# The first seven rows of a row-sum kernel, loaded in two transfers over 32 and 96 partitions

## The chip, the core and the metric

The kernel runs on one core of a Trainium2 chip. The core has 128 on-chip memory partitions and several engines with instruction streams of their own: VectorE (DVE in the profile), ScalarE (ACT), GpSimd (POOL), TensorE (PE, not used here) and SyncE (SP), which issues most transfers. Transfers are carried out by 16 DMA engines. The metric is the time of one execution on the device in microseconds (us); for a single core this is the core's own time.

## The reference

The input `x` is 32 x 512 x 1024 float32 (67.1 MB), the output the sum over its last axis, 32 x 512 float32 (65.5 KB).

```python
def reference(x: np.ndarray) -> np.ndarray:
    return np.sum(x, axis=-1).astype(np.float32)
```

So every element is read once and added once; there are 16,384 row sums of 1,024 elements.

## The kernel before

**Tiling.** The 16,384 rows are spread over the 128 partitions, 128 rows (`J`) for each. They form two blocks: `x_b`, of which each partition has 112 consecutive rows (`LONG`), and `x_a`, of which each has 16 (`BIG`). `rows_from(j, n)` gives the rows `j` to `j + n - 1` of every partition; since the rows of one partition follow each other in memory, one load of `n` rows takes one run of `n` x 4,096 bytes for each partition. Row sums are collected in `sums` (128 x 128) and stored in three parts at the end.

**Stages.** Twelve loads go through three buffers of sixteen rows each (`inpool`, `bufs=3`):

1. the first load: rows 0 to 6 of `x_b` over all 128 partitions, 28,672 B for each (`FIRST = 7`, line 212);
2. seven loads of sixteen rows, 65,536 B for each partition (loop of lines 215 to 224): first the block `x_a`, then rows 16 to 111 of `x_b`;
3. the rest of the first sixteen rows: six rows (line 227), two rows (line 228), and one row in two pieces of 560 and 464 elements (lines 236 and 237).

The first load and the first six of stage 2 are reduced by a single VectorE instruction each (`vec`, line 152). For the last sixteen-row load and the six and two rows, VectorE and ScalarE share the rows: VectorE folds a row's halves (`halves`, line 166), ScalarE sums while copying (`act`, line 179). VectorE alone sums the last row from its two pieces.

**What sets the order.** The schedule is written by hand (`tc.manual_schedule()`): each engine runs its instructions in program order. All loads are issued by SyncE, by line 191 in the helper `rows` and by lines 236 and 237. What each waits for:

- The very first SyncE load is moved by `issue_first_load_at_entry` ahead of the barrier with which the program begins; it must wait for nothing.
- The next load (`k == 0`) is held until `ready`, a small ScalarE activation (line 206), has ended; the code gives as a reason that no second load is to be issued while the first one's descriptors are made.
- The load of `k == 1` is held until the first reduction (`first`) has ended.
- Each later load waits until its buffer is free, that is until the load and the reduction that used it three loads before are done.

`order_waits` sorts the waits of instructions that have several, and `wait_for_the_store_at_the_clear` moves the wait for the last store; neither is touched by the change.

Of the kernel before, what the change touches and what calls it, by code (L numbers as in the profile page):

```python
# [100 lines left out]
@with_exitstack  # L101
def kernel(
    ctx: ExitStack,
    tc: tile.TileContext,
    x: bass.AP,
    out: bass.AP,
):
    nc = tc.nc
    nc.at_finalize(issue_first_load_at_entry)
    nc.at_finalize(order_waits)  # L110
    nc.at_finalize(wait_for_the_store_at_the_clear)
    fp32 = mybir.dt.float32
    P = 128
    batch, seq, dim = x.shape
    rows = batch * seq
    J = rows // P
    BIG = 16

    LONG = J - BIG
    rows_in = x.flatten_outer_dims()
    rows_out = out.rearrange("b s -> (b s)")
    x_a = rows_in[: P * BIG].rearrange("(p j) d -> p j d", p=P)
    x_b = rows_in[P * BIG :].rearrange("(p j) d -> p j d", p=P)
    out_a = rows_out[: P * BIG].rearrange("(p j) -> p j", p=P)
    out_b = rows_out[P * BIG :].rearrange("(p j) -> p j", p=P)


    def rows_from(j, n):
        return x_b[:, j : j + n, :] if j < LONG else x_a[:, j - LONG : j - LONG + n, :]

    last = 0
    FIRST = 7
    pieces = (560, 464)
    LINE = 64

    with (
        tc.tile_pool(name="small", bufs=1) as smallpool,  # L140
        tc.tile_pool(name="in", bufs=3) as inpool,
        tc.tile_pool(name="unread", bufs=4, space=bass.MemoryType.PSUM) as upool,
        tc.tile_pool(name="stage", bufs=1) as stpool,
        tc.manual_schedule(),
    ):


        seed = smallpool.tile([P, LINE // 2], fp32)
        sums = stpool.tile([P, J], fp32)

        def vec(dst, src):
            return nc.vector.tensor_reduce(  # L152
                out=dst, in_=src, axis=mybir.AxisListType.X, op=mybir.AluOpType.add
            )

        def hold(inst, until, reason):
            tc.add_manual_dep(
                inst.ins,
                until.ins.name,
                mybir.DependencyInfo(mybir.DependencyClass.Sync, mybir.DependencyReason.DATA),  # L160
                reason=reason,
            )

        def halves(dst, src):
            n = src.shape[-1] // 2
            return nc.vector.tensor_tensor_reduce(  # L166
                out=src[:, :n],
                in0=src[:, :n],
                in1=src[:, n:],
                scale=1.0,  # L170
                scalar=0.0,
                op0=mybir.AluOpType.add,
                op1=mybir.AluOpType.add,
                accum_out=dst,
            )

        def act(dst, src, n):
            unread = upool.tile([P, dim], fp32)
            nc.scalar.activation(  # L179
                out=unread[:, :n],  # L180
                in_=src,
                func=mybir.ActivationFunctionType.Copy,
                accum_out=dst,
            )

        sums_of = []

        def rows(t, a, n, j, n_act, pairs=False):
            nv = n - n_act
            block = t[:, a * dim : (a + n) * dim].rearrange("p (n d) -> p n d", d=dim)  # L190
            load = nc.sync.dma_start(out=block, in_=rows_from(j, n))  # L191
            if pairs:
                for q in range(nv):
                    sums_of.append(halves(sums[:, j + q : j + q + 1], block[:, q, :]))
            else:
                sums_of.append(vec(sums[:, j : j + nv], block[:, :nv, :]))
            for q in range(nv, n):
                act(sums[:, j + q : j + q + 1], block[:, q, :], dim)
            return load

        def store(eng, dst, j0, j1):
            return eng.dma_start(out=dst, in_=sums[:, j0:j1])

        nc.vector.memset(seed[:, :1], 0.0)  # L204
        unread = upool.tile([P, dim], fp32)
        ready = nc.scalar.activation(  # L206
            out=unread[:, :1], in_=seed[:, :1], func=mybir.ActivationFunctionType.Copy
        )

        j = last  # L210
        t = inpool.tile([P, BIG * dim + LINE], fp32)
        rows(t, 0, FIRST, j, 0)
        first = sums_of[-1]
        wholes = [LONG, *range(BIG, LONG, BIG)]
        for k, at in enumerate(wholes):
            t = inpool.tile([P, BIG * dim + LINE], fp32)
            if k < len(wholes) - 1:
                load = rows(t, 0, BIG, at, 0)
            else:
                rows(t, 0, BIG, at, 7, pairs=True)  # L220
            if k == 0:
                hold(load, ready, "no second load while the first one's descriptors are made")
            if k == 1:
                hold(load, first, "no descriptors of later loads while the first ones start")

        t = inpool.tile([P, BIG * dim + LINE], fp32)
        rows(t, FIRST, 6, j + FIRST, 2, pairs=True)
        two = rows(t, FIRST + 6, 2, j + FIRST + 6, 1, pairs=True)
        a = BIG - 1

        j += a
        c, width = pieces
        whole = t[:, a * dim + c : BIG * dim + 2]
        nc.vector.memset(whole[:, width + 1 :], 0.0)  # L234
        part = t[:, a * dim : a * dim + c]
        nc.sync.dma_start(out=part, in_=rows_from(j, 1)[:, 0, :c])  # L236
        nc.sync.dma_start(out=whole[:, :width], in_=rows_from(j, 1)[:, 0, c:])
        late = "its packets come behind those of the loads"
        hold(store(nc.scalar, out_b[:, BIG:], BIG, LONG), two, late)
        hold(store(nc.scalar, out_a, LONG, J), two, late)  # L240
        halves(whole[:, width : width + 1], part)
        halves(sums[:, j : j + 1], whole)
        store(nc.sync, out_b[:, :BIG], 0, BIG)
# [30 lines left out]
```

## Time and profile before

| what | value |
|---|---|
| three runs | 161.17, 161.21, 161.32 us; median 161.21 us |
| profiled execution | span 159.5 us from the first to the last instruction (the profile gives no other time for this execution) |
| VectorE busy | 120.6 us, 76% of the span |
| ScalarE busy | 12.1 us, 8% |
| mean transfer rate over the span | 421 GB/s |
| bytes read from device memory | 67.11 MB |
| first load, issue to landing | 11.0 us |

How to read it. Times in the profile start at the first instruction, which here is the issue of the first load. "SPq" is the queue of SyncE, "PEq" that of TensorE; L191 is line 191 of the kernel. An instruction in the timeline has its start, its length and, in brackets, how long its engine was idle before it and what ended that idle time. The chain of waits follows the work that ended last back from the end, at each step to what released it. A window lists the busy time of each engine in a stretch, the share of the DMA engines and the rate in GB/s. Busy shares are averages over the whole span; what bounds a stage is read from the wait that ends last in it.

### The profile page before, as it was taken

Reading aid. Unit: us, or ns where it says so; the run is one execution under the profiler, and the core shown is the slowest. Engines: PE = TensorE matmul, PEld = TensorE weight load, DVE = VectorE, ACT = ScalarE, POOL = GpSimd, SP = SyncE. Lnnn points to the kernel's source line nnn. Section 1 sums busy time; section 2 is a strip of 40 time slices with the busy share of each in tenths; the row PEclk is TensorE's granted clock in tenths of the full one; section 3 lists DMA queues with packets and bytes.
Section 4 is the critical chain, followed back from the end, with each engine's and each line's share of the span. In section 5 each row is a group of like instructions: output and inputs, shape, how many; then the busy total and the mean of one; then the engine's idle time right before and its main releaser. Section 6 shows DMA issues by size and latency. Waiting matters only on the chain.

```text
span 159.5 us, 135 instructions
## 1 busy us (share of the span) xinstructions
DVE 120.6 (76%) x41; ACT 12.1 (8%) x22; POOL 0.2 (0%) x4
## 2 busy tenths in 40 slices
DVE  0029600499995999769996899949999499994955
ACT  3000000000000000000000000000000000003993
POOL 0000000000000000000000000000000000000000
DMA  8899899699699699699699798996996996996993
GB/s 302 388 493 526 362 427 526 296 493 526 263 526 526 263 526 526 263 526 493 296 526 444 345 526 378 411 526 296 493 526 263 526 526 263 526 526 265 425 382 128
DMA packets 2160, 67.18 MB, mean 421 GB/s; under 512 B 624, under 2 KB 752, under 8 KB 880
## 3 DMA queue, kind: packets, MB, share of 16 engines
q1 hardware_dynamic: 1872, 67.12, 97.8%
q10 hardware_dynamic: 288, 0.06, 0.2%
HBM read 67.11 MB, written 0.07 MB: 421 GB/s over the span
## 4 chain that ended last, share of the span: by engine, by line
DMA 71%; DVE 27%; SPq 1%; issue 0%; DVEq 0%
DMA t<-in_x_dram 71%; DVE sums L152 26%; SPq L191 0%; SPq L236 0%; DVE t L166 0%; DVEq L269 0%
## 5 line engine op out<-in xcount | busy, mean ns | idle before, releaser
L152 DVE TENSOR_REDUCE sums<-t 128x16 f32<-128x16384 f32 (+1 forms) x7 | 110.9, 15849 | 32.3 <-DMA t<-in_x_dram 32.3
L179 ACT ACTIVATE unread<-t 128x1024 f32<-128x1024 f32 x10 | 10.1, 1011 | 144.3 <-DMA t<-in_x_dram 144.3
L166 DVE CUSTOM_DVE_ANT_0 t<-t 128x512 f32<-128x512 f32 (+2 forms) x16 | 9.6, 654 | 4.0 <-DMA t<-in_x_dram 4.0
L179 ACT ACTIVATION_READ_ACCUMULATOR unread<-t 128x1 f32 x10 | 1.9, 188 | 0.0
L206 ACT ACT_TABLE_LOAD x1 | 1.3, 1283 | 0.8 <-PEq L258 0.8
L166 DVE DVE_READ_ACCUMULATOR2_ANT sums<- 128x1 f32 x15 | 1.2, 82 | 0.0
L204 DVE MEMSET seed<- 128x1 f32 x1 | 0.1, 59 | 0.8 <-PEq L258 0.8
L206 ACT ACTIVATE unread<-seed 128x1 f32<-128x1 f32 x1 | 0.2, 174 | 0.0
L258 POOL MEMSET const-bfloat16-1.0<- 128x1 bf16 x1 | 0.1, 102 | 0.0
L258 POOL MEMSET const-uint8-127<- 128x1 uint8 x1 | 0.1, 102 | 0.0
L258 POOL MEMSET const-float32-0.0<- 128x1 f32 x1 | 0.1, 99 | 0.2 <-issue 0.2
L258 POOL MEMSET const-float32-1.0<- 128x1 f32 x1 | 0.1, 99 | 0.0
L166 DVE DVE_READ_ACCUMULATOR2_ANT t<- 128x1 f32 x1 | 0.1, 83 | 0.0
L234 DVE MEMSET t<- 128x1 f32 x1 | 0.1, 59 | 0.0
## 6 DMA issues: line engine op xcount, KB each, us to landing
t<-in_x_dram SPq DMA_DIRECT2D x1, 3584.0 KB, 11.0
t<-in_x_dram SPq DMA_DIRECT2D x1, 3072.0 KB, 28.7
t<-in_x_dram SPq DMA_DIRECT2D x1, 1024.0 KB, 30.7
t<-in_x_dram SPq DMA_DIRECT2D x1, 280.0 KB, 31.0
t<-in_x_dram SPq DMA_DIRECT2D x1, 232.0 KB, 31.1
t<-in_x_dram SPq DMA_DIRECT2D x7, 40.7
out_dram<-sums ACTq DMA_DIRECT2D x1, 48.0 KB, 1.6
out_dram<-sums ACTq DMA_DIRECT2D x1, 8.0 KB, 1.6
```

Source lines behind the costliest of these rows:

```text
L152: return nc.vector.tensor_reduce(out=dst, in_=src, axis=mybir.AxisListType.X, op=mybir.AluOpType.add)
L166: return nc.vector.tensor_tensor_reduce(out=src[:, :n], in0=src[:, :n], in1=src[:, n:], scale=1.0, scalar=0.0, op0=mybir.AluOpType.add, op ...
L179: nc.scalar.activation(out=unread[:, :n], in_=src, func=mybir.ActivationFunctionType.Copy, accum_out=dst,)
L204: nc.vector.memset(seed[:, :1], 0.0)
L206: ready = nc.scalar.activation(out=unread[:, :1], in_=seed[:, :1], func=mybir.ActivationFunctionType.Copy)
L234: nc.vector.memset(whole[:, width + 1 :], 0.0)
L258: nc = _bacc.Bacc("TRN2", target_bir_lowering=False, num_devices=1)
```

## The change

The first load, of rows 0 to 6, is split by partitions: one load over partitions 0 to 31 and another over 32 to 127, with the same 28,672 B for each partition. The first of the two is now the one that is issued at the entry. The second takes over the wait for `ready` that the first sixteen-row load (`k == 0`) had, and that load now has no wait of its own and is issued directly behind. The reduction of the seven rows stays one VectorE instruction over all 128 partitions and waits for both loads. The hold of `k == 1` on this reduction stays.

```diff
         j = last
         t = inpool.tile([P, BIG * dim + LINE], fp32)
-        rows(t, 0, FIRST, j, 0)
-        first = sums_of[-1]
+        block = t[:, : FIRST * dim].rearrange("p (n d) -> p n d", d=dim)
+        few = 32
+        nc.sync.dma_start(out=block[:few], in_=rows_from(j, FIRST)[:few])
+        other = nc.sync.dma_start(out=block[few:], in_=rows_from(j, FIRST)[few:])
+        hold(other, ready, "no second load while the first one's descriptors are made")
+        first = vec(sums[:, j : j + FIRST], block)
+        sums_of.append(first)
         wholes = [LONG, *range(BIG, LONG, BIG)]
         for k, at in enumerate(wholes):
             t = inpool.tile([P, BIG * dim + LINE], fp32)
...
                 rows(t, 0, BIG, at, 7, pairs=True)
-            if k == 0:
-                hold(load, ready, "no second load while the first one's descriptors are made")
             if k == 1:
                 hold(load, first, "no descriptors of later loads while the first ones start")
```

SyncE's order of issue is then: the load over 32 partitions (entry), the load over 96 partitions (after `ready`), the sixteen-row loads, and everything behind as before.

## The prediction

> **What bounds the kernel now.** I read the chain of waits first, because it says which work ends last at each step; then the first microseconds of the timeline and of the windows, because the change lies there; then the DMA queues and SyncE's own waits. The chain (start us, duration us, what), in part:
>
> ```profile
> 0.00 11.01 DMA t<-in_x_dram
> ...
> 11.03 7.63 DVE sums L152
> ...
> 18.68 30.92 DMA t<-in_x_dram
> ...
> 126.16 31.13 DMA t<-in_x_dram
> ...
> 157.32 0.40 DVE t L166
> ```
>
> The share of 26.4% that this chain gives to L152 misleads: it names the reductions because a load's issue waits for them, while the timeline shows VectorE waiting for data ahead of every one of them:
>
> ```profile
> 0.00 19.48 SPq L191 DMA_DIRECT2D t<-in_x_dram  x4
> ...
> 2.06 0.17 ACT L206 ACTIVATE unread<-seed 128x1 f32<-128x1 f32 x1
> 11.03 7.62 DVE L152 TENSOR_REDUCE sums<-t 128x7 f32<-128x7168 f32 x1 [10.14 <-DMA t<-in_x_dram]
> 30.30 17.22 DVE L152 TENSOR_REDUCE sums<-t 128x16 f32<-128x16384 f32 x1 [11.65 <-DMA t<-in_x_dram]
> ...
> 49.62 17.22 DVE L152 TENSOR_REDUCE sums<-t 128x16 f32<-128x16384 f32 x1 [2.10 <-DMA t<-in_x_dram]
> ...
> 126.90 17.22 DVE L152 TENSOR_REDUCE sums<-t 128x16 f32<-128x16384 f32 x1 [2.10 <-DMA t<-in_x_dram]
> ```
>
> Sixteen-row loads land at 30.30 and 126.90 and four times between, so one takes (126.90 - 30.30)/5 = 19.32 us; it carries 128 x 65,536 B = 8.39 MB, which is 434 GB/s. All 67.11 MB at that rate are 154.6 us of the span of 159.5. The other 4.9 us lie at the two ends: the first load's landing at 11.01 where 3.67 MB at 434 GB/s are 8.45 (2.56 more), and 2.2 us from the last landing at 157.30 to the end. In between the stream has no hole: (30.30 - 11.03) = 19.27 us for the second load, too. So **the transfers bound the kernel, and what delays their stream at the start moves the end by as much**: VectorE, with 17.22 us of work for 19.32 us of load, can't give time back or take it.
>
> The start, in windows (window, length, busy us of DVE, ACT, POOL, clock, DMA share, GB/s):
>
> ```profile
> 0.50:1.00 0.50, 0.06 (x1) 0.24 (x1) 0.00 (x0) 1.00 0.23 57
> 1.00:1.50 0.50, 0.00 (x0) 0.50 (x1) 0.00 (x0) 1.00 3.34 860
> 1.50:2.00 0.50, 0.00 (x0) 0.50 (x1) 0.00 (x0) 1.00 0.00 0
> 2.00:2.50 0.50, 0.00 (x0) 0.22 (x2) 0.00 (x0) 1.00 0.00 0
> 2.50:3.00 0.50, 0.00 (x0) 0.00 (x0) 0.00 (x0) 1.00 1.87 803
> 3.00:3.50 0.50, 0.00 (x0) 0.00 (x0) 0.00 (x0) 1.00 0.27 115
> ```
>
> 57 and 860 GB/s over 0.5 us are 0.459 MB, that is 16 pieces of 28,672 B (one partition's seven rows); so are 803 and 115. The view counts a packet whole where it starts. So the 16 DMA engines each start a packet of one partition about 1.0 to 1.5 us after the issue at 0.00, a second one at 2.5 to 3.5, and one each 8.45/8 = 1.06 us from there. The first takes about half a microsecond to one more than the others.
>
> ```profile
> q1 hardware_dynamic: 1872, 67.12, 97.8%
> ...
> SPq L191 <- DVE sums L152: 102.2, 6, 17.2
> ...
> SPq L191 <- ACT unread L206: 1.5, 1, 1.5
> ```
>
> The queue's packets (number, MB, share) fill 97.8% of 16 engines' span: 67.12 MB/(0.978 x 159.5 us x 16) = 26.9 GB/s for each engine. The last line is the wait before SyncE's second load: it goes out at 2.26, when ScalarE's L206 has ended (2.06 + 0.17).
>
> **The change part by part.** *The first load, split.* The load at 0.00 now carries 32 x 28,672 B = 0.92 MB instead of 3.67; the 96 other partitions (2.75 MB) are a load of their own. By number of packets nothing changes: 32 packets are two for each of 16 engines and 96 are six, if both loads go over all engines, eight as before. At full rate the small load occupies 0.92 MB/434 GB/s = 2.11 us, and from the first packets' end at about 2.7 (1.0, plus 1.06, plus the 0.6 of the start) its second packets end at about 3.75.
>
> *The added issue.* SyncE issues the second load at 2.26, behind the same wait on L206 that the first sixteen-row load had. Its first packets can start at 2.26 + 1.0 = 3.3 by the first load's row, 0.45 before the queue would run dry: hidden. If that cover went, each tenth late would be a tenth at the end. The sixteen-row load goes out directly behind, at about 2.6 instead of 2.26 (one issue is 0.33 us); its bytes are wanted only at about 10, so 0.35 us cost nothing. But it no longer waits until the load before it has started, as it did. Above, this costs at most what the wait was worth, 1.5 us less the 0.45 of cover, about 1; below, nothing. I take 0, because the two loads issued together at 18.68 leave no hole in the landings.
>
> *The reduction.* L152's 7.62 us now waits for both loads. The load of k == 1 waits for it: were the landing 4.2 us late, it would go out at 22.9 instead of 18.68, with the load in flight landing at 34.5 instead of 30.30. Cushion 11.6 us, as before. Later waits move along; the added load shifts each later load to the next completion semaphore, whose former user landed long before. Tail: unchanged, 2.2 us.
>
> *Which partitions.* What no row of this trace shows is a load over fewer than 128 partitions: is 434 GB/s the rate of 16 engines whatever they write, or of the way into 128 partitions? In the second case each partition's way must take its 524,288 B at its share of 434 GB/s, which is the whole 154.6 us, so the time in which part of these ways get nothing is added to the end. The small load leads the queue, and the packets of the 96 stand behind it on the same engines. If 32 partitions get a share f of the rate, it takes 2.11/f us, and the ways not used sit idle for all of it. Ends: f = 1, nothing is lost, 0; f = 1/4, 32 of 128 ways exactly, +8.45 us. Below nothing: at most the 0.5 us by which the first packets are stretched, if fewer packets made them start better. No row stands nearer to one end than to the other; every load of the page has f = 1 by shape. I take the middle in ratio, f = 1/2: 2.11/0.5 = **+4.2 us**, and keep both ends.
>
> [...]
>
> **Sum.** Span 159.5 + 4.2 + 0 (issue) + 0 (reduction, tail) = 163.7. The page gives the span alone for that execution; the median of the three runs is 161.21, so 1.7 us lie around the span, unchanged: **165.4 us**. The crowding can be worse than idle ways: two thirds of the 96 belong to the idle half, and where their six packets on one engine meet another engine's, each takes up to 2.1 us instead of 1.06. I allow up to +3 for it, so this case's own range is +2.5 to +7: 163.7 to 168.2.
>
> **The rivals.** *All engines at full rate (not slower).* The limit is each engine's 26.9 GB/s, wherever it writes; 16 x 26.9 = 430 explains the whole rate without any other limit, which speaks for it. The packets then follow without a hole and the landing stays at 11.0: 161.2; with a better first round, up to 0.5 us less, 160.7. It decides if the small load's second packets end before about 4.3. Against it: nothing here, but nothing tests it.
>
> *Engines bound to partitions.* Eight packets of each load on each engine fit a fixed set of eight partitions for each, too. Then 32 partitions use only four to eight engines, and the others get their first packet from the load issued at 2.26 instead of 0.00. They still have eight packets to move, so the end is 2.26 later: 161.2 + 2.26 = 163.5. For it: the regular rounds of 16; against it: the 0.92 MB divide evenly over 16 engines.
>
> *A quarter of the rate:* +8.45, 169.7, if the ways are one for each four or eight partitions in sequence.
>
> *Late packets:* the sixteen-row load's issue at 2.6 disturbs the start of the 96: up to +1, 162.2.
>
> **How the numbers follow.** Half rate 0.40, fixed engines 0.20, all at full rate 0.27, a quarter 0.07, late packets 0.06. The likeliest gives 165.4. The range leaves out the quarter, some of the gain and the worst crowding: 160.9 to 167.6. A measurement tells about 0.2% (0.3 us) from no change. Full rate splits into 0.14 for faster (the first round improves), 0.11 for the same, 0.02 for slower; all others are slower: 0.40 + 0.20 + 0.07 + 0.06 + 0.02 = 0.75.
>
> **What would show it.** Right: the first two loads land together at about 15, L152's 7.62 us starts there, every landing behind is 4.2 later, 19.3 apart as before, and the windows up to about 5.8 us show packets starting at half the pace. Fixed engines: the packets of the first window are fewer than 16 and a second group starts at 3.3. Wrong altogether: the first reduction still starts at 11.0.

## The result and the profile after

The changed kernel takes 169.22 us (169.15 to 169.34, five runs) against 161.21 (161.17 to 162.0): the ratio is 1.049, with a 95% interval of 1.047 to 1.051. That is 8.0 us more. The forecast was 165.4, with a range up to 167.6; the sign was right, the loss nearly twice as large. The profiled span went from 159.5 to 167.4 us. Some single executions of kernels below lie far above the others of the same kernel (188.1 us with the middle first, 175.8 and 187.7 us with two queues), and the ratios leave them out.

VectorE's first reductions after the change, from the timeline (start, length, in brackets the idle time before):

```profile
19.41 7.62 DVE L152 TENSOR_REDUCE sums<-t 128x7 f32<-128x7168 f32 x1 [18.49 <-DMA t<-in_x_dram]
38.40 17.22 DVE L152 TENSOR_REDUCE sums<-t 128x16 f32<-128x16384 f32 x1 [11.37 <-DMA t<-in_x_dram]
57.68 17.22 DVE L152 TENSOR_REDUCE sums<-t 128x16 f32<-128x16384 f32 x1 [2.06 <-DMA t<-in_x_dram]
```

They stood at 11.03, 30.30 and 49.62. So the first reduction is 8.4 us late, the next two 8.1; from there the landings are 19.3 us apart as before, and the span ends 7.9 later. Everything was lost ahead of the first reduction. The page's second part (40 equal slices of the span, 4.2 us each after the change and 4.0 before) shows in what way, first before the change and then after it:

```profile
DMA  8899899699699699699699798996996996996993
GB/s 302 388 493 526 362 427 526 296 493 526 263 526 526 263 526 526 263 526 493 296 526 444 345 526 378 411 526 296 493 526 263 526 526 263 526 526 265 425 382 128
```

```profile
DMA  9999969997997999699969997997999599969994
GB/s 219 219 219 219 454 298 501 501 407 345 501 501 329 423 501 501 266 486 501 454 298 501 501 407 345 501 501 313 439 501 501 251 501 501 454 298 439 435 383 137
```

In the first four slices after the change, to 16.7 us, the DMA engines are as busy as ever, but they move 219 GB/s, half of 434. It is not only the first two microseconds' worth of data, the small load, that goes at half pace. The windows count a packet whole where it starts (window, length, busy us of DVE, ACT and POOL, clock, DMA share, GB/s):

```profile
1.00:1.50 0.50, 0.00 (x0) 0.50 (x1) 0.00 (x0) 1.00 3.71 860
1.50:2.00 0.50, 0.00 (x0) 0.50 (x1) 0.00 (x0) 1.00 0.21 57
...
2.50:3.00 0.50, 0.00 (x0) 0.00 (x0) 0.00 (x0) 1.00 1.63 344
3.00:3.50 0.50, 0.00 (x0) 0.00 (x0) 0.00 (x0) 1.00 1.95 401
3.50:4.00 0.50, 0.00 (x0) 0.00 (x0) 0.00 (x0) 1.00 0.84 172
4.00:4.50 0.50, 0.00 (x0) 0.00 (x0) 0.00 (x0) 1.00 0.00 0
4.50:5.00 0.50, 0.00 (x0) 0.00 (x0) 0.00 (x0) 1.00 0.80 172
5.00:5.50 0.50, 0.00 (x0) 0.00 (x0) 0.00 (x0) 1.00 2.01 459
5.50:6.00 0.50, 0.00 (x0) 0.00 (x0) 0.00 (x0) 1.00 1.24 287
```

860 + 57 over half a microsecond are 0.459 MB, sixteen packets of 28,672 B: all 16 engines start a packet of the small load in the first round. 344 + 401 + 172 are again sixteen, its second round, and 172 + 459 + 287 the first round of the 96 partitions. The rounds are now about 2.1 us apart, where before it was 1.06, and they stay so: 3.67 MB at 219 GB/s are 16.8 us instead of 8.45, which is 8.3 of the 8.4 us. By share, the small load takes 0.92 MB/219 = 4.2 instead of 2.1 us, and **the 96 partitions 2.75 MB/219 = 12.6 instead of 6.3**.

The packet records of the traces, which hold the start and the length of every packet, give it for each engine. The two packets of the small load take 4.18 us together; the first two packets took 2.85 before, since the first of them was stretched at the start. The six packets of the 96 take 12.53 instead of 6.38 us. The first packet of the sixteen-row load behind them takes 2.86 instead of 2.42 us. That is 1.33 + 6.15 + 0.44 = 7.92 us, against 7.9 in the span. The two loads landed apart, 7.0 and 17.0 us after their issues at 0.00 and 2.28, as the page lists them (KB, us to landing):

```profile
t<-in_x_dram SPq DMA_DIRECT2D x1, 2688.0 KB, 17.0
...
t<-in_x_dram SPq DMA_DIRECT2D x1, 896.0 KB, 7.0
```

### The profile page after: what moved, and what is told of

It is laid out like the page before. It is cut to its first block, busy times and chain, and to the rows that moved or that the text cites. A ratio compares the mean times of both kernels' runs of the same rounds, so it can differ in the third digit from the quotient of the medians.

```text
span 167.4 us, 138 instructions
## 1 busy us (share of the span) xinstructions
DVE 120.6 (72%) x41; ACT 12.1 (7%) x22; POOL 0.2 (0%) x4
## 4 chain that ended last, share of the span: by engine, by line
DMA 71%; DVE 25%; ACT 1%; SPq 1%; issue 0%; DVEq 0%
DMA t<-in_x_dram 71%; DVE sums L152 25%; ACT L206 1%; SPq L191 0%; SPq L239 0%; DVE t L166 0%; ACT unread L206 0%; DVEq L152 0%; DVEq L272 0%
## 6 DMA issues: line engine op xcount, KB each, us to landing
t<-in_x_dram SPq DMA_DIRECT2D x7, 40.6
```

## The experiments

Three theories. A: the partitions that a load writes set its pace, and it matters which ones they are. The ways in, and engines that share one, are the author's supposition in this theory; no trace here records a way, and the runs show the pace of each set of partitions alone. B: any load over fewer than 128 partitions goes at half pace, whichever they are. C: the start is disturbed by the added issue and the moved wait, the rival "late packets" of the prediction. Edits are given against the changed kernel or the kernel before, as said. Kernels that ran once (those from "Far from the start" on, except the change with its second load cut and the one with two queues) are compared with the kernel before on the same chip (161.2 to 161.3 us).

### Split by rows instead of partitions

Against the changed kernel:

```diff
-        few = 32
-        nc.sync.dma_start(out=block[:few], in_=rows_from(j, FIRST)[:few])
-        other = nc.sync.dma_start(out=block[few:], in_=rows_from(j, FIRST)[few:])
+        few = 2
+        nc.sync.dma_start(out=block[:, :few], in_=rows_from(j, few))
+        other = nc.sync.dma_start(out=block[:, few:], in_=rows_from(j + few, FIRST - few))
```

> The first seven rows again in two loads with the same waits, but split by rows: two rows and then five, each over all 128 partitions. Theory A (the partitions written set the pace: a load over part of the partitions makes pairs of engines share a way in): no partial load, so about 161.2 us, first reduction at about 11. Theory B (any load over fewer than 128 partitions runs at half pace, whichever they are): also 161.2. Theory C (the added issue and the moved wait at the start cost the time): about 169, as the changed kernel.

161.13 us; ratio to the kernel before 0.9995 (0.9984 to 1.0006). Two loads, the added issue, the moved wait and the sixteen-row load directly behind are all still there, and the loss is gone; the first reduction starts where it did before:

```profile
10.93 7.62 DVE L152 TENSOR_REDUCE sums<-t 128x7 f32<-128x7168 f32 x1 [10.02 <-DMA t<-in_x_dram]
30.20 17.22 DVE L152 TENSOR_REDUCE sums<-t 128x16 f32<-128x16384 f32 x1 [11.65 <-DMA t<-in_x_dram]
```

Theory C falls: the cost of splitting and of the moved wait is nothing that can be measured. It also shows that the smaller first transfer brings nothing by itself.

### 64 and 64

```diff
-        few = 32
+        few = 64
```

> The change with 64 and 64 partitions instead of 32 and 96. Theories A and B: both halves at half pace, eight rounds of 2.1 us instead of 1.06, so about 169 us, as with 32. If only the small load ran at half pace and the other at full, a load of 64 would cost twice what one of 32 does, and the time would lie between. Theory C: 169.

170.37 us, ratio 1.057 (1.055 to 1.058). As A and B expect, though 1.1 us more than with 32 and 96; its packets take 2.19 us on average against 2.09 there, and why is not shown.

### The middle first

Against the changed kernel:

```diff
-        nc.sync.dma_start(out=block[:few], in_=rows_from(j, FIRST)[:few])
-        other = nc.sync.dma_start(out=block[few:], in_=rows_from(j, FIRST)[few:])
-        hold(other, ready, "no second load while the first one's descriptors are made")
+        nc.sync.dma_start(out=block[32:96], in_=rows_from(j, FIRST)[32:96])
+        for lo, hi in ((0, 32), (96, 128)):
+            other = nc.sync.dma_start(out=block[lo:hi], in_=rows_from(j, FIRST)[lo:hi])
+            hold(other, ready, "no second load while the first one's descriptors are made")
```

> The first load over partitions 32 to 95, then one over 0 to 31 and one over 96 to 127. [...] Theory A with the partitions dealt out in blocks of 32, or theory B: the full loss, about 169. Theory C, with one more issue: 169 or a little more.

165.9 us, ratio 1.029 (1.027 to 1.030): half of the loss, with one load more. The author's guess for theory A was 165.2 us: the 64 in the middle at full pace, the two loads of 32 at half. It came out, and B falls. The windows before and after 6 us of this kernel:

```profile
1.00:6.00 5.00, 0.06 (x1) 1.46 (x2) 0.00 (x0) 1.00 0.95 367
6.00:14.00 8.00, 0.00 (x0) 0.00 (x0) 0.00 (x0) 1.00 1.02 229
```

The first five microseconds hold 1.835 MB, the 64 packets of the middle load: four rounds, the first stretched as before and the others at the full pace (1.07 us for a packet). Then the two loads of 32 go at 229 GB/s.

### Far from the start

Against the kernel before, sixteen-row loads are issued in parts; `rows` has an argument `ranges` for it:

```diff
-            load = nc.sync.dma_start(out=block, in_=rows_from(j, n))
+            for lo, hi in ranges:
+                load = nc.sync.dma_start(out=block[lo:hi], in_=rows_from(j, n)[lo:hi])
...
+        split = {
+            2: ((0, 32), (32, 128)),
+            3: ((0, 64), (64, 128)),
+            4: ((32, 96), (0, 32), (96, 128)),
+            5: ((0, 96), (96, 128)),
+        }
```

> The kernel before, with four of its sixteen-row loads split by partitions in the middle of the stream, far from the start: k = 2 as 0-31 and 32-127, k = 3 as 0-63 and 64-127, k = 4 as 32-95, 0-31 and 96-127, k = 5 as 0-95 and 96-127. Before, each of them took 19.3 us. Theory A: 38.7 us each for k = 2, 3 and 5, and 29.0 for k = 4 (9.7 for the middle 64, 9.7 each for the two of 32); in all some 68 us more, near 229 us. Theory B: 38.7 for all four, near 239 us. Theory C (a matter of the start): 19.3 for all, 161.

234.76 us, 6 more than theory A had. Each reduction starts when its load has landed, so the differences of these starts are the loads' lengths:

```profile
49.96 17.22 DVE L152 TENSOR_REDUCE sums<-t 128x16 f32<-128x16384 f32 x1 [2.50 <-DMA t<-in_x_dram]
89.71 17.22 DVE L152 TENSOR_REDUCE sums<-t 128x16 f32<-128x16384 f32 x1 [22.54 <-DMA t<-in_x_dram]
130.33 17.22 DVE L152 TENSOR_REDUCE sums<-t 128x16 f32<-128x16384 f32 x1 [23.40 <-DMA t<-in_x_dram]
160.44 17.22 DVE L152 TENSOR_REDUCE sums<-t 128x16 f32<-128x16384 f32 x1 [12.89 <-DMA t<-in_x_dram]
...
200.32 17.22 DVE L152 TENSOR_REDUCE sums<-t 128x16 f32<-128x16384 f32 x1 [22.66 <-DMA t<-in_x_dram]
```

39.75, 40.62, 30.11 and 39.88 us for `k` = 2 to 5, against 38.7, 38.7, 29.0 and 38.7 of theory A. The loss belongs to the transfers, not to the start, and half pace is a little less than half (20.3 for 64 partitions against 19.3).

### The change with its second load cut

Against the changed kernel:

```diff
-        other = nc.sync.dma_start(out=block[few:], in_=rows_from(j, FIRST)[few:])
-        hold(other, ready, "no second load while the first one's descriptors are made")
+        for lo, hi in ((few, 96), (96, P)):
+            other = nc.sync.dma_start(out=block[lo:hi], in_=rows_from(j, FIRST)[lo:hi])
+            hold(other, ready, "no second load while the first one's descriptors are made")
```

> The change with its second load of 96 partitions cut into 32 to 95 and 96 to 127; the small load over 0 to 31 stays first. Theory A: the small load costs 2.1 us more than at full pace, 96 to 127 the same, the 64 in the middle nothing: +4.2 to +4.7, about 165.7 us, though one more load is issued; so 3.5 us of the change's 8.0 lie in how the 96 are dealt to the engines. If the small load at the head of the queue costs the time by itself, whatever follows: 169.

165.66 us, ratio 1.027 (1.025 to 1.029). The small load leads the queue unchanged, and 3.6 us are back. Two loads of 32 cost 4.4 us here, 2.2 each if they cost alike. How the 96 are dealt to the engines it does not show.

### Where it is written, or where it is read

Against the kernel before; `ranges` has as a third number the partition whose rows the first one written receives:

```diff
+        split = {
+            2: ((0, 64, 32), (64, 96, 0), (96, 128, 96)),
+            3: ((32, 96, 0), (0, 32, 64), (96, 128, 96)),
+        }
```

> The kernel before, with two sixteen-row loads split in the middle of the stream so that the partitions written and the rows read are not the same ones (the output's rows are exchanged between partitions thereby): k = 2 writes 0-63 from the rows of 32-95, then 64-95 and 96-127; k = 3 writes 32-95 from the rows of 0-63, then 0-31 and 96-127. If the partitions written decide: 39 to 41 us for k = 2 and 29 to 30 for k = 3. If the place of the rows in the device memory decides: the other way round.

```profile
50.14 17.22 DVE L152 TENSOR_REDUCE sums<-t 128x16 f32<-128x16384 f32 x1 [2.68 <-DMA t<-in_x_dram]
90.45 17.22 DVE L152 TENSOR_REDUCE sums<-t 128x16 f32<-128x16384 f32 x1 [23.09 <-DMA t<-in_x_dram]
120.20 17.22 DVE L152 TENSOR_REDUCE sums<-t 128x16 f32<-128x16384 f32 x1 [12.53 <-DMA t<-in_x_dram]
```

192.99 us in all; 40.3 us for `k` = 2, 29.75 for `k` = 3: the partitions written decide, the place of the rows in device memory does not.

### Sixteen, 112 and 48 partitions

Against the kernel before, with `split = {2: ((0, 16), (16, 128)), 4: ((16, 80), (80, 128), (0, 16))}`.

> The kernel before, with k = 2 as 0-15 and 16-127, and k = 4 as 16-79, 80-127 and 0-15, far from the start. [...] If any partial load simply runs at half pace: 39 for both.

218.75 us in all; 41.0 us for `k` = 2 (reductions at 50.16 and 91.12) and 53.2 for `k` = 4 (112.26 and 165.46). One half pace for all (39 and 39) is out: `k` = 4 takes 14 us more, and 80 to 127 took 8.1 to 8.5 us a packet there instead of 2.42, a factor of 3.4. How partitions are dealt to the engines is not shown by this.

### Two queues

Against the run with 64 and 64: the second half from ScalarE's queue, with the hold on `ready` also back on the load of `k == 0`.

```diff
-        other = nc.sync.dma_start(out=block[few:], in_=rows_from(j, FIRST)[few:])
+        other = nc.scalar.dma_start(out=block[few:], in_=rows_from(j, FIRST)[few:])
...
+            if k == 0:
+                hold(load, ready, "no second load while the first one's descriptors are made")
```

> The change with 64 and 64 partitions, the second half issued by ScalarE's queue instead of SyncE's, behind the same wait. Theory A: on each engine the packets of the two halves may now alternate. If an engine works on one packet of each queue at a time, the two halves use different ways and the loss falls, from 170.4 us toward 161 to 165. If it takes a whole packet of one queue and then of the other, pairs meet as before: 169 to 170.

Ratio 1.058 (1.055 to 1.061), some 170.6 us: no gain. The half on ScalarE's queue landed 24.7 us after its issue and the first reduction started at 27.49. By the packet records this half was issued at 2.7 us, but none of its packets starts before 9.7, when the first engines are through with the other half; from 14 us on, its rounds take turns with those of the sixteen-row load. So the second queue did not let the halves run side by side, and what they would cost if they did is not shown.

### Unread loads: which partitions, and what one shape costs

Seven runs add one load to the kernel before, of nine rows that nothing reads, between the first two sixteen-row loads:

```diff
         first = sums_of[-1]
+        spare = t[:, FIRST * dim : BIG * dim].rearrange("p (n d) -> p n d", d=dim)
...
                 hold(load, ready, "no second load while the first one's descriptors are made")
+                lo, hi = 32, 96
+                nc.sync.dma_start(out=spare[lo:hi], in_=rows_from(BIG, BIG - FIRST)[lo:hi])
```

Only `lo, hi` differ in the others. The expectations are those for 32 to 95, 36 to 99, 48 to 95, 80 to 127, 40 to 103, 48 to 111 and 32 to 127, in this order. Theories A1 and A2, for 40 to 103 and 48 to 111, take it that only some of the engines share a way there; that is a supposition of the author, which no run shows.

> The kernel before, with one load more that nothing reads: nine rows (36,864 B for each partition) into partitions 32 to 95, queued between the first two sixteen-row loads; so its whole length is added. Theory A: four packets for each engine at full pace, 4 x 1.36 = 5.4 us; about 166.7 us, and the windows stay at 434 GB/s.

> The same unread load into partitions 36 to 99, shifted by four. [...]

> The same unread load into 48 partitions, 48 to 95. [...]

> The same unread load into 48 partitions, 80 to 127, as many as in the run before. [...] If the number of partitions decides and not which ones: the same as 48 to 95.

> [...] Theory A1 (engines that share a way hold up the others as soon as there are a few of them): all 16 slow down, and in the 11 us that the load then takes the windows fall toward 220 to 300 GB/s. Theory A2 (only the engines that share slow down; over 32 to 127 all of them shared): the windows stay near 434 GB/s for the first 5.5 us of the load, as with 36 to 99.

> [...] Theory A1: all 16 at half pace, windows at about 220 GB/s for 11 us. [...]

> The same into the 96 partitions of the change, 32 to 127, alone in the stream: six packets for each engine. At full pace 6 x 1.36 = 8.2 us (169.4); at the half pace that the changed kernel showed, 6 x 1.36 x 2.1 = 17.1 us, 178. That the 96 take twice their time without the small load ahead of them would show that the larger part of the loss is theirs.

| partitions | time, us | added | expected | at full pace |
|---|---|---|---|---|
| 32 to 95 | 166.68 | 5.5 | 5.4 | 5.4 |
| 36 to 99 | 175.20 | 14.0 | 10.9 | 5.4 |
| 40 to 103 | 172.71 | 11.4 | 11 | 5.4 |
| 48 to 111 | 172.55 | 11.3 | 11 | 5.4 |
| 48 to 95 | 169.35 | 8.2 | 8.6 | 4.1 |
| 80 to 127 | 174.97 | 13.8 | 13.9 | 4.1 |
| 32 to 127 | 177.47 | 16.2 | 17.1 | 8.2 |

Of the expected figures, 10.9 and 11 are four packets at half pace (4 x 1.36 x 2), 8.6 is three (3 x 1.36 x 2.1), and 13.9 is three at the factor that 80 to 127 had far from the start (3 x 1.36 x 3.4). Which of these paces a shape would have was the author's estimate, from a supposition on the engines and the ways that no run shows.

The unread load starts at about 29 us in each. Windows of 32 to 95, then of 36 to 99, of 40 to 103 and of 48 to 111:

```profile
29.00:32.00 3.00, 1.74 (x1) 0.00 (x0) 0.00 (x0) 1.00 0.91 393
```

```profile
29.00:32.00 3.00, 1.28 (x1) 0.00 (x0) 0.00 (x0) 1.00 0.98 381
32.00:35.00 3.00, 3.00 (x1) 0.00 (x0) 0.00 (x0) 1.00 1.01 381
35.00:38.00 3.00, 3.00 (x1) 0.00 (x0) 0.00 (x0) 1.00 0.99 306
38.00:41.00 3.00, 3.00 (x1) 0.00 (x0) 0.00 (x0) 1.00 1.00 309
```

```profile
32.00:35.00 3.00, 3.00 (x1) 0.00 (x0) 0.00 (x0) 1.00 1.04 209
35.00:38.00 3.00, 3.00 (x1) 0.00 (x0) 0.00 (x0) 1.00 1.04 209
```

```profile
32.00:35.00 3.00, 3.00 (x1) 0.00 (x0) 0.00 (x0) 1.00 1.08 221
35.00:38.00 3.00, 3.00 (x1) 0.00 (x0) 0.00 (x0) 1.00 1.01 209
```

The mean length of a packet can be worked out from such a line: share x 16 engines x 3 us, divided by the number of packets that the rate stands for. In the first line 393 GB/s are 32 packets of 36,864 B, so one takes 0.91 x 48/32 = 1.36 us.

With 36 to 99 the rate stays at 381 GB/s for the first six microseconds of the load, a little under the full 434. In the packet records 56 of the 64 packets take 1.36 to 1.46 us, and the other eight, 2.25 to 4.54 us long, form two chains of four, which are two engines; the other 14 are hardly held up. With 40 to 103 the rate is 209, half, and none of the 64 packets is spared: they take 1.90 to 2.96 us. 48 to 111 (221 and 209) is no worse. So for these two shapes A1 had the rate (220 to 300, and about 220) and A2 did not (434 for the first 5.5 us with 40 to 103): all 16 engines slow down. Whether they do because a few of them share a way is not shown, nor why the step lies between 36 to 99 and 40 to 103. The two runs with 48 partitions differ by 5.6 us, so it is the place of the partitions, and not their number, that decides. The 96 of the change, alone in the stream, take twice their time.

The 14.0 us for 36 to 99 were a miss: 10.9 were expected. The windows at 35 to 41 us show 306 and 309 GB/s, when the next sixteen-row load has begun. In the packet records one packet of that load then takes 7.37 us, three times its usual 2.42, the packets of the two late engines take 3.6 to 4.5 us, and the next load's packets on the other engines about 3.0. So 36 to 99 holds 381 GB/s where 40 to 103 and 48 to 111 hold 209 to 221, and still costs the most of the four loads of 64 partitions, because the load ends with its two slowest engines.

## Why the prediction went wrong in size

- **The transfers bound the kernel, and a delay at their start moves the end by as much: right.** The first reduction is 8.4 us late, the end 7.9; the landings stay 19.3 apart.
- **The added issue, the wait, the reduction and the tail at nothing: right.** The split by rows keeps all of them and gives 0.9995.
- **The small load at half pace: right.** All 16 engines take part, and its two rounds take 4.2 us. Its loss was put a little too high: before the change the first two rounds took 2.85 us and not 2.1, so its own packets lose 1.3 us. The first two loads were to land together at about 15; they landed at 7.0 and 19.3.
- **The step that failed is the time of the 96 partitions.** The prediction added 4.2 us because "the ways not used sit idle for all of it". On its own assumption that lets the 96 go on at the pace that the fuller half of the ways allows: 64 of them on half of the ways, 8.45 us instead of 6.3, so 2.1 of the 4.2. For anything worse it said "I allow up to +3 for it", where a packet meets another engine's; with all of that it came to 168.2, still under the result. Measured were 12.5 us for the 96 in the changed kernel, 6.1 more than before, and by themselves 16.2 instead of 8.2 with nine rows, which is 8.0 x 7/9 = 6.2. That the partitions written set the pace was right (no loss by rows, 8.0 us by partitions); the term was mis-sized by some 4 us (6.1 against 2.1). No run shows ways, an idle half of them, or packets that meet there. What stands in their place: every packet of the 96 goes at half pace (1.92 to 2.24 us instead of 1.06). Why all of them do is not shown.
- **The rivals.** "All engines at full rate" fell with the result. "Engines bound to partitions" fell with the first round of 16 packets. "Late packets" fell with the split by rows. "A quarter of the rate" gave 169.7, the number nearest to the result, by a wrong mechanism: the small load ran at 219 GB/s, not at 109, and most of the loss lies in the 96.

What the runs show is a pace for each set of partitions. At full pace: 32 to 95 (5.5 us added, 5.4 at full pace). At half: 0 to 31 and 96 to 127 (229 GB/s instead of 434), 0 to 63 and 64 to 127 (40.6 us together instead of 19.3), 40 to 103 and 48 to 111 (209 to 221 GB/s), 32 to 127 (16.2 us added instead of 8.2).

Open: which engine carries which partition is not in the profile, and neither is what lies between the engines and the partitions; the author's suppositions on both remain suppositions, and the cause of these paces is not shown. The step between 36 to 99 (381 GB/s) and 40 to 103 (209) stands on one execution of each kernel.

## What to carry to other kernels

Split a load by rows, not by partitions: the same two transfers cost 0 us by rows and 8 us by partitions. When part of the partitions must be loaded, what counts is which ones: 32 to 95 ran at the full pace (5.5 us added, 5.4 at full pace), 0 to 63 and 64 to 127 at half (40.6 us together instead of 19.3). In a kernel that is bound by its transfers, price every load of a changed step, not only the new one: the larger share of this loss, 6.15 of 7.92 us, lay in the load that looked harmless.

## What was not expected of the hardware

36 to 99 leaves the rate at 381 GB/s with two slow engines, 40 to 103 brings all 16 engines down to 209, and 48 to 111 is no worse (221 and 209). In time 36 to 99 cost more, 14.0 us against 11.4 and 11.3. 48 partitions cost 8.2 us at 48 to 95 and 13.8 at 80 to 127. The DMA share said nothing of the pace: the busy digits of the first four slices are 9 at 219 GB/s, and were 8 and 9 at 302 to 526 before, so the two rows are to be read together.
